# A decoder block on one core: sums, splits and the first gate put elsewhere in the mixing stage, one scaling moved to ScalarE

## The chip, the core and the metric

The kernel runs on one core of a Trainium2 chip. A core has TensorE (PE, matrix products; its weight loads are listed apart as PEld), VectorE (DVE), ScalarE (ACT), GpSimd (POOL) and SyncE (SP, which here issues nearly all DMA transfers). Each engine takes its instructions in order and waits for others through semaphores. Sixteen DMA engines move data between the chip's memory and the core's own.

The metric is the device time of one execution in microseconds (us), as the median of several runs. Beside it stands one profiled execution, from which all rows below come; a time such as "at 288.05" is counted from the start of that execution's span.

## What is computed

One decoder layer on 256 tokens of 1024 channels, in float32: a gated feed-forward network, a mixing layer of two branches, a second feed-forward network, a norm. Cut to what matters:

```python
h = h + 0.5 * swiglu(rmsnorm(h, ffn1_norm), ffn1_w_gate, ffn1_w_up, ffn1_w_down)
n = rmsnorm(h, mix_norm)
z = n @ w_in                         # q, k, v (512 each), u, gv (512 each)
attn = moba_attention(q, k, v)       # 8 heads of 64; 256 tokens are one block: causal softmax
zg = gelu(z[..., 3 * 512:])
gm = u * (tril(w_s) @ layernorm(gv) + b_s)      # by groups, inside chunks of 128 tokens
gates = sigmoid(n @ w_gate + b_gate)            # 2 x 1024 columns
merged = gates[:, :1024] * (attn @ w_branch_attn) + gates[:, 1024:] * (gm @ w_branch_gmlp)
h = h + merged @ w_out
h = h + 0.5 * swiglu(rmsnorm(h, ffn2_norm), ffn2_w_gate, ffn2_w_up, ffn2_w_down)
return rmsnorm(h, final_norm)
```

## The kernel before

**Split products.** A float32 product is made of three passes: each operand is split into a high part (rounded by a cast) and a low part (the rest), and high by high, high by low and low by high are summed in PSUM (`mm3`, L253). For the weights this is done on the chip. A weight *unit* comes as two *halves* of 512 KB. A half is loaded into a `raw` tile (`fetch_to`, L173; DMA on SP's queue), cast on ACT into the unit's tile `w` (L260), and its low part is subtracted on DVE (L262). I call the two steps *cast* and *low*. There are 7 raw tiles and 5 unit tiles, used in turn: the load of a half waits for the low of the half 7 before it, and a cast waits until PE has done with the unit 5 before it.

`split_half` (L185) takes the next half in the fixed order of units: it asks for loads up to six halves ahead, emits the cast, and either emits the low at once or, with `later=True`, returns it as a function that the caller runs at its own place. `unit(i, ahead)` (L221) takes halves until unit `i + ahead` is split, and then asks for one more load.

**Fewer products.** Some stages use sums of weight blocks so that seven products do the work of eight (`seven`, L385). Their units come in pairs: a "single" unit, and a "sums" unit that has no load of its own: four additions on DVE (L209 to L212) make its two halves from the raw tiles of the single one, which are then cast and lowered like others. `uvs` is such a stage: units `muv` to `muv + 3` hold the first half of u's and v's weights. The sums unit `muv + 3` is the last of them.

**Order.** From L752 on, the order of the program's text is the order on ACT and DVE (`in_order`), and it is so on PE and SP everywhere. A wait of one instruction holds all behind it on its engine. DMA transfers are issued by SP in the same way, in the order in which the text asks for them, loads of weights among them.

**The mixing stage** (L962 to L1067) runs, on PE, the products of q, k and gv, those of u and v, the scores (L863), the spatial products (L912), four *gate* chunks of 48 matmuls each (`chunk(mg, ...)`), the attention products (`attend`, L937), and two merges (`merge`, L1037), each with the gmlp branch (pg, L1041) and the attention branch (pa, L1052). Behind them stands the output product (`down_features`, acc, L229 and L234). On the other engines, in this stage:

- `turn_qk` (L845) scales q or k on ACT and turns it on DVE. The turned rows go to memory and come back in another layout (`qk_way`).
- `layer_norm(j)` (L949) on DVE, behind gv's gelu on ACT.
- `exponents(j)` (L873): maxima on DVE, exponents and their sums on ACT, for row tile j of 128 queries and 8 heads; tile 0 has 128 keys, tile 1 has 256.
- `probabilities(j, sm)` (L884): reciprocal of the sums, scaling of the whole tile (L890) and its turning (L893), all on DVE.
- `to_keys(j)` (L896) sends the turned probabilities to memory in four transfers, `by_keys(j)` (L901) brings them back by keys.
- `gated(i)` (L915): the spatial gating of half of the columns on DVE, and its turning; it leaves through `gm_way` and comes back as `gm_back`, from which `settle_in(gmT, gm_back)` (L1019) makes gm's high part on ACT and low part on DVE.
- `gate(g, ps, splits)` (L926): `2 * splits` halves are cast first, then for both row tiles gate g is scaled and added to its bias on DVE (L931) and put through the sigmoid on ACT (L933), then the lows run.
- `va` (L1007): v scaled on ACT.
- In `merge`, DVE multiplies by the gates (L1043, L1054), adds (L1055) and turns (L1056); the turned rows leave through `m_way`, come back, and `settle` (L1032) makes the high and low parts (mg) that the output product takes.

The gate units are `mg` to `mg + 7`. Behind them come the branches' units (gmlp, attention, gmlp, attention: `mb` to `mb + 3`) and the four of the output. Before the change, the halves of unit `mg + 5` are cast in `gate(0, psg, 1)`, those of `mg + 7` in `gate(1, ..., 1)`, those of `mb + 1` (the first attention branch) in `gate(2, ..., 1)`; the others by the `unit` calls of the chunks.

Of the kernel before, what the change touches and what calls it, by code (L numbers as in the profile page):

```python
# [10 lines left out]
F32 = mybir.dt.float32  # L11
F32R = mybir.dt.float32r
BF16 = mybir.dt.bfloat16
AF = mybir.ActivationFunctionType
# [4 lines left out]
P = 128  # L19
D = 1024  # L20
S = 256
NT = S // P
# [3 lines left out]
HEADS = 8  # L26
# [27 lines left out]
def block_kernel(ctx, tc, t, out):  # L54
    nc = tc.nc
# [84 lines left out]
    muv = len(units)  # L140
# [44 lines left out]
    def split_half(later=False):  # L185

        i, hf = divmod(done_to[0], 2)
        if hf == 0:
            unit_tile(i)
        fetch_to(done_to[0] + RAW)  # L190
        done_to[0] += 1
        if kind(i):
            return quarters(i, hf)
        w, sl = parts[i], half(i, hf)
        return split(w[:, sl, 0, :], w[:, sl, 1, :], raws.pop((i, hf)), later)

    def quarters(i, hf):

        w = parts[i]
        if kind(i) == "single":  # L200
            r = raws[i, hf].rearrange("p one (n c) -> p (one n) c", c=512)
            r, to = (r, w[:, 1:3]) if hf else (r[:, :1], w[:, :1])
        else:
            if hf == 0:
                (a, b), (c, d) = ([r[:, 0, n:n + 512] for n in (0, 512)] for r in [raws.pop((i - 1, k)) for k in range(2)])
                for k in range(2):
                    raws[i, k] = sump.tile([P, 2, 512], F32, tag="sum", name=f"sum{i}_{k}")
                first, second = raws[i, 0], raws[i, 1]
                nc.vector.tensor_add(first[:, 0], a, b)  # L209
                nc.vector.tensor_add(first[:, 1], b, d)  # L210
                nc.vector.tensor_add(second[:, 0], first[:, 0], d)
                nc.vector.tensor_add(second[:, 1], second[:, 0], c)  # L212
            r, to = raws.pop((i, hf)), w[:, 2 * hf:2 * hf + 2]
        return split(to[:, :, 0, :], to[:, :, 1, :], r)

# [356 lines left out]
    def by_token(way):  # L572
        return way.rearrange("(j p) a n -> p j (a n)", p=P)
# [178 lines left out]
    with in_order():  # L752
# [92 lines left out]
        def turn_qk(i, ps):  # L845
            by_tokens = tokens(mix_a[:, 8 + 4 * i:12 + 4 * i])
            for j in range(NT):
                nc.scalar.activation(by_tokens[:, j], ps[j], AF.Copy, scale=rs2[j])
                nc.vector.transpose(qk_turned[i][:, j], by_tokens[:, j])
# [33 lines left out]

        def probabilities(j, sm):  # L884


            n, pr = (j + 1) * P, prob[j]
            ri = small.tile([P, HEADS], F32, tag="ri", name=f"ri{j}")
            nc.vector.reciprocal(ri, sm)
            nc.vector.tensor_mul(pr, pr, ri[:, :, None].to_broadcast([P, HEADS, n]))  # L890
            turned.append(mix_a[:, 2 * KB:2 * KB + 4, :] if j == 0 else
                          act.tile([P, KB, S], F32, tag="nC", name="turned1"))
            nc.vector.transpose(turned[j].rearrange("p b (h c) -> p b h c", c=32),  # L893
                                pr.rearrange("p h (b c) -> p b h c", c=32))

        def to_keys(j):  # L896
            for b in range(4):
                nc.sync.dma_start(on_way[j][:, b, :].rearrange("(k r) n -> r k n", r=32),
                                  turned[j][32 * b:32 * (b + 1)])
# [23 lines left out]
            for j in range(NT):  # L923
                nc.vector.transpose(gm_turned[j][:, i * S:(i + 1) * S], m[:, j])

        def gate(g, ps, splits=0):  # L926

            c = slice(g * 512, (g + 1) * 512)
            lows = [split_half(True) for _ in range(2 * splits)]
            for j in reversed(range(NT)):  # L930
                nc.vector.scalar_tensor_tensor(gates[:, j, c], ps[j], rs2[j], gates[:, 0, c],  # L931
                                               op0=ALU.mult, op1=ALU.add)
                nc.scalar.activation(gates[:, j, c], gates[:, j, c], AF.Sigmoid)  # L933
            for low in lows:
                low()

# [28 lines left out]
        turn_qk(0, psq)  # L965
        chunk(mk, nT2, "k", 0, [1], psk, 3, DEEP)
        nc.sync.dma_start(by_token(qk_way[0]), qk_turned[0])
        turn_qk(1, psk)
        nc.sync.dma_start(by_token(qk_way[1]), qk_turned[1])
        q_back = tmp.tile([P, S // 32, P], F32, tag="back", name="qback", bufs=1)  # L970
# [25 lines left out]
        spatial()  # L996
        psg = chunk(mg, nT2, "g", 0, [0])
        nc.sync.dma_start(gates[:, 0, :], t["b_gate"].to_broadcast([P, 2 * D]))
        sums = [exponents(j) for j in range(NT)]
        gated(0)  # L1000
        probabilities(0, sums[0])
        to_keys(0)
        chunk(mg, nT2, "g", 0, [1], psg)
        probabilities(1, sums[1])
        gated(1)
        for j in range(NT):
            nc.scalar.activation(va[:, j, :], psv[j], AF.Copy, scale=rs2[j])  # L1007
        to_keys(1)
        by_keys(0)
        for j in range(NT):  # L1010
            nc.sync.dma_start(by_token(gm_way)[:, j], gm_turned[j])
        gate(0, psg, 1)
        psg = chunk(mg, nT2, "g", 1, [0])
        by_keys(1)
        gm_back = tmp.tile([P, S // 32, P], F32, tag="back", name="gmback", bufs=1)
        from_way(gm_back, gm_way)
        gate(1, chunk(mg, nT2, "g", 1, [1], psg), 1)
        gate(2, chunk(mg, nT2, "g", 2), 1)
        settle_in(gmT, gm_back)  # L1019
        gate(3, chunk(mg, nT2, "g", 3))  # L1020

# [221 lines left out]
```

## Time and profile before

| | |
|---|---|
| runs | 516.11, 516.30, 516.36 us |
| median | 516.3 us |
| the profiled execution | 516.4 us |
| its span | 514.7 us |
| mean granted clock of PE | 0.993 |

The span runs from the first to the last instruction; the 1.7 us around it are the execution's start and end. A row of a timeline gives start, length, engine, line of the program, operation, what it writes and reads, its shape and how many of the kind follow one another; a bracket at the end gives the engine's idle time before it and what ended it. A row of a group (with a bar) gives busy time, mean length in ns, and idle time before the group. A row of a stretch gives its bounds and length, then the busy time and number of instructions of PE, PEld, DVE, ACT and POOL, the granted clock of PE, the share of the 16 DMA engines that was busy, and GB/s. "SPq" is SP's queue of transfers: the time of a row is that of their issue, not of the landing.

### The profile page before, as it was taken

What the parts mean: (1) busy time and instruction counts of PE and PEld (TensorE: products, weight loads), DVE (VectorE), ACT (ScalarE), POOL (GpSimd) and SP (SyncE); (2) the same over time, 40 slices, a digit from 0 to 9 for tenths busy, and PEclk for the clock granted to TensorE, in tenths of its full rate; (3) what the DMA queues carried; (4) which work ended last, traced back from release to release, by engine and by line L of the source; (5) the groups of instructions that cost most, each with busy time, mean ns of one, the idle gap of its engine ahead of it and who ended that gap; (6) DMA issues with size and microseconds to landing.
All of it is one profiled execution on the core that took longest, in us unless ns stands there. A gap on an engine that the chain in (4) does not pass through costs nothing.

```text
span 514.7 us, 6830 instructions
## 1 busy us (share of the span) xinstructions
PE 505.0 (98%) x2314; PEld 418.7 (81%) x2314; DVE 462.1 (90%) x675; ACT 309.9 (60%) x444; POOL 11.2 (2%) x25
## 2 busy tenths in 40 slices
PE   9999999999999999999999999999999999999995
PEld 6888888888888888888888877888888888888884
DVE  6898999999997989799894876998989989999995
ACT  7985549646564766765952803768635756565533
POOL 0010000000000010000000000001000000000001
PEclk9999999999999999999999998999999999999998
DMA  8998588798765987786789765937789648998402
GB/s 317 375 330 327 156 276 258 267 307 280 228 220 179 308 282 291 184 291 245 232 218 304 287 202 171 295 120 260 257 274 300 213 140 274 350 327 251 177 1 82
DMA packets 63987, 126.82 MB, mean 246 GB/s; under 512 B 11729, under 2 KB 36817, under 8 KB 63825
## 3 DMA queue, kind: packets, MB, share of 16 engines
q1 hardware_dynamic: 63664, 126.06, 74.4%
q8 instruction: 18, 0.29, 0.3%
q10 hardware_dynamic: 288, 0.33, 0.2%
q14 instruction: 17, 0.13, 0.1%
HBM read 113.26 MB, written 13.11 MB: 246 GB/s over the span
## 4 chain that ended last, share of the span: by engine, by line
PE 94%; DVE 2%; DMA 2%; issue 1%; ACT 1%; SPq 0%; POOLq 0%; DVEq 0%; POOL 0%; ACTq 0%
PE f L255 12%; PE f L257 12%; PE f L256 12%; PE accdown L257 4%; PE accdown L255 4%; PE accdown L256 4%; PE acch L257 3%; PE acch L255 3%; PE acch L256 3%; PE acc L229 3%; PE g L255 3%; PE g L256 3%; PE g L257 3%; PE acc L234 1%; PE accuv L256 1%; PE accuv L257 1%
## 5 line engine op out<-in xcount | busy, mean ns | idle before, releaser
L262 DVE TENSOR_TENSOR w<-raw,w 128x1024 fp32r<-128x1024 f32 (+1 forms) x180 | 202.7, 1163 | 18.0 <-ACT w L260 17.6
L260 ACT CAST w<-raw 128x1024 fp32r<-128x1024 f32 (+1 forms) x180 | 173.2, 1007 | 31.4 <-DMA raw<-in_ba 8.3
L257 PE MATMUL f<-w,n 128*128 128x512 f32 x272 | 105.8, 389 | 0.0
L255 PE MATMUL f<-w,n 128*128 128x512 f32 x272 | 105.8, 389 | 0.0
L256 PE MATMUL f<-w,n 128*128 128x512 f32 x272 | 105.8, 389 | 0.0
L257 PEld LDWEIGHTS f<-w,n 128*128 128x128 f32 x272 | 51.1, 188 | 10.7
L256 PEld LDWEIGHTS f<-w,n 128*128 128x128 f32 x272 | 51.1, 188 | 10.6
L255 PEld LDWEIGHTS f<-w,n 128*128 128x128 f32 x272 | 51.1, 188 | 10.5
L260 ACT CAST w<-sum 128x1024 fp32r<-128x1024 f32 x34 | 35.8, 1052 | 37.6 <-DVE sum L210 29.5
L262 DVE TENSOR_TENSOR w<-sum,w 128x1024 fp32r<-128x1024 f32 x34 | 41.0, 1216 | 0.5 <-ACT w L260 0.5
L256 PE MATMUL accdown<-w,f1h 128*128 128x512 f32 x68 | 26.5, 389 | 0.0
L257 PE MATMUL accdown<-w,f1h 128*128 128x512 f32 x68 | 26.5, 389 | 0.0
L255 PE MATMUL accdown<-w,f1h 128*128 128x512 f32 x68 | 26.5, 389 | 0.0
L255 PE MATMUL g<-w,n 128*128 128x512 f32 x64 | 25.0, 391 | 0.0
L257 PE MATMUL g<-w,n 128*128 128x512 f32 x64 | 24.9, 389 | 0.0
L256 PE MATMUL g<-w,n 128*128 128x512 f32 x64 | 24.9, 389 | 0.0
L256 PE MATMUL acch<-w,f2h 128*128 128x512 f32 x59 | 23.0, 389 | 0.0
L257 PE MATMUL acch<-w,f2h 128*128 128x512 f32 x59 | 23.0, 389 | 0.0
L255 PE MATMUL acch<-w,f2h 128*128 128x512 f32 x59 | 23.0, 389 | 0.0
L229 PE MATMUL acc<-mg,w 128*128 128x512 f32 x64 | 18.7, 420 | 2.2 <-DVE mg L262 2.2
L596 ACT ACTIVATE f2s<-f,rstd 128x256 f32<-128x256 f32 x18 | 8.2, 474 | 14.0 <-PE f L257 13.9
L229 PEld LDWEIGHTS acc<-mg,w 128*128 128x128 f32 x64 | 12.2, 205 | 4.2 <-DVE mg L262 2.4
(291 smaller groups left out, 917.0 us busy)
## 6 DMA issues: line engine op xcount, KB each, us to landing
raw<-in_f SPq DMA_DIRECT2D x72, 512.0 KB, 6.5
raw<-in_f2d SPq DMA_DIRECT2D x22, 512.0 KB, 6.8
raw<-in_gate SPq DMA_DIRECT2D x16, 512.0 KB, 5.9
raw<-in_f1s SPq DMA_DIRECT2D x14, 512.0 KB, 6.4
raw<-in_f1d SPq DMA_DIRECT2D x14, 512.0 KB, 5.0
raw<-in_out SPq DMA_DIRECT2D x8, 512.0 KB, 5.3
raw<-in_f2s SPq DMA_DIRECT2D x6, 512.0 KB, 6.7
f1way<-f1t SPq DMA_DIRECT2D x11, 256.0 KB, 6.3
```

Source lines behind the costliest of these rows:

```text
L229: nc.tensor.matmul(ps, st, both.rearrange("p two n -> p (two n)"), start=first, stop=last)
L234: nc.tensor.matmul(ps[:, n:], st, both[:, 0, :], start=False, stop=False)
L255: nc.tensor.matmul(ps, sh, mh, start=first, stop=False)
L256: nc.tensor.matmul(ps, sh, ml, start=False, stop=False)
L257: nc.tensor.matmul(ps, sl, mh, start=False, stop=last)
L260: nc.scalar.copy(hi, src)
L262: nc.vector.tensor_sub(lo, src, hi.bitcast(F32))
L596: nc.scalar.activation(sg, ps[j][:, :CH], AF.Silu, scale=rs[j])
```

## The change

1. The four additions for the sums unit `muv + 3` become a function, `quarter_sums`, and are called by hand between k's product and k's turning; before, they were emitted behind the turning, with the split of that unit.
2. `probabilities(j)` keeps the reciprocal and the scaling. For tile 1 the scaling is eight activations on ACT, one for each head, in place of one multiplication on DVE. The turning is a function of its own, `turn(j)`.
3. `gate` is cut into `gate_in` (scaling and bias, DVE) and `gate_out` (sigmoid, ACT). For gate 0, `gate_in` stands ahead of the second tile's turning, and `gate_out` behind its way to the keys and ahead of `va`.
4. The halves of `mg + 4` are cast ahead of the exponents, those of `mg + 5` ahead of the second tile's scaling; their lows run behind the first and the second turning. `gate(2)` takes no halves any more, so the two of `mb + 1` are split with the next chunk, behind `settle_in` of gm.
5. `to_keys(1)` stands ahead of `va`.

```diff
+    def quarter_sums(i):
+        (a, b), (c, d) = ([r[:, 0, n:n + 512] for n in (0, 512)] for r in [raws.pop((i - 1, k)) for k in range(2)])
+        for k in range(2):
+            raws[i, k] = sump.tile([P, 2, 512], F32, tag="sum", name=f"sum{i}_{k}")
+        first, second = raws[i, 0], raws[i, 1]
+        nc.vector.tensor_add(first[:, 0], a, b)
+        nc.vector.tensor_add(first[:, 1], b, d)
+        nc.vector.tensor_add(second[:, 0], first[:, 0], d)
+        nc.vector.tensor_add(second[:, 1], second[:, 0], c)
...
-            if hf == 0:
...
+            if hf == 0 and (i, 0) not in raws:
+                quarter_sums(i)
...
-            n, pr = (j + 1) * P, prob[j]
+            pr = prob[j]
             ri = small.tile([P, HEADS], F32, tag="ri", name=f"ri{j}")
             nc.vector.reciprocal(ri, sm)
-            nc.vector.tensor_mul(pr, pr, ri[:, :, None].to_broadcast([P, HEADS, n]))
+            if j:
+                for hd in range(HEADS):
+                    nc.scalar.activation(pr[:, hd, :], pr[:, hd, :], AF.Copy, scale=ri[:, hd:hd + 1])
+            else:
+                nc.vector.tensor_mul(pr, pr, ri[:, :, None].to_broadcast([P, HEADS, P]))
+
+        def turn(j):
+
+            pr = prob[j]
             turned.append(mix_a[:, 2 * KB:2 * KB + 4, :] if j == 0 else
...
-        def gate(g, ps, splits=0):
+        def gate_in(g, ps):
 
             c = slice(g * 512, (g + 1) * 512)
-            lows = [split_half(True) for _ in range(2 * splits)]
             for j in reversed(range(NT)):
                 nc.vector.scalar_tensor_tensor(gates[:, j, c], ps[j], rs2[j], gates[:, 0, c],
                                                op0=ALU.mult, op1=ALU.add)
+
+        def gate_out(g):
+
+            c = slice(g * 512, (g + 1) * 512)
+            for j in reversed(range(NT)):
                 nc.scalar.activation(gates[:, j, c], gates[:, j, c], AF.Sigmoid)
+
+        def gate(g, ps, splits=0):
+
+            lows = [split_half(True) for _ in range(2 * splits)]
+            gate_in(g, ps)
+            gate_out(g)
             for low in lows:
                 low()
...
         nc.sync.dma_start(by_token(qk_way[0]), qk_turned[0])
+        quarter_sums(muv + 3)
         turn_qk(1, psk)
...
+        lows = [split_half(True) for _ in range(2)]
         sums = [exponents(j) for j in range(NT)]
         gated(0)
         probabilities(0, sums[0])
+        turn(0)
         to_keys(0)
+        for low in lows:
+            low()
         chunk(mg, nT2, "g", 0, [1], psg)
+        lows = [split_half(True) for _ in range(2)]
         probabilities(1, sums[1])
         gated(1)
+        gate_in(0, psg)
+        turn(1)
+        to_keys(1)
+        for low in lows:
+            low()
+        gate_out(0)
         for j in range(NT):
             nc.scalar.activation(va[:, j, :], psv[j], AF.Copy, scale=rs2[j])
-        to_keys(1)
         by_keys(0)
         for j in range(NT):
             nc.sync.dma_start(by_token(gm_way)[:, j], gm_turned[j])
-        gate(0, psg, 1)
         psg = chunk(mg, nT2, "g", 1, [0])
...
-        gate(2, chunk(mg, nT2, "g", 2), 1)
+        gate(2, chunk(mg, nT2, "g", 2))
         settle_in(gmT, gm_back)
         gate(3, chunk(mg, nT2, "g", 3))
```

More of the change, by code (lines that the diff above doesn't have):

```diff
@@ L203, in quarters @@
         else:
-            if hf == 0:
[L205 to L212, printed above, removed]
+            if hf == 0 and (i, 0) not in raws:
+                quarter_sums(i)
             r, to = raws.pop((i, hf)), w[:, 2 * hf:2 * hf + 2]
```

## The prediction

> **What bounds the kernel now.** I read the busy table first, then the rows in which TensorE (PE) idles, then the chain that released it, then the queues behind that chain.
>
> ```profile
> PE 505.0 (98%) x2314; PEld 418.7 (81%) x2314; DVE 462.1 (90%) x675; ACT 309.9 (60%) x444; POOL 11.2 (2%) x25
> ```
>
> PE is the bound, so a change to DVE, ACT or the queues pays only where PE waits. PE's timeline has one such place after the start (start, length, then idle before it):
>
> ```profile
> 307.50 0.28 PE L257 MATMUL pa<-w,ao 128*128 128x256 f32 x1
> 309.98 2.50 PE L229 MATMUL acc<-mg,w 128*128 128x512 f32 x5 [2.20 <-DVE mg L262]
> ```
>
> After the second merge's last matmul PE waits 2.20 us for the first settled block of the merged rows. The stretches around it (PE busy behind the first comma, granted clock third from the end) add a second cost:
>
> ```profile
> 306.27:309.68 3.41, 1.50 (x13) 1.30 (x11) 0.18 (x1) 0.62 (x2) 0.00 (x0) 1.00 0.59 134
> ```
> ```profile
> 309.68:313.09 3.41, 3.11 (x7) 2.48 (x8) 2.72 (x7) 2.10 (x5) 0.00 (x0) 0.50 0.81 235
> ```
>
> For the 3.41 us after the wait the clock is halved. Seven matmuls fill 3.11 us, 0.43 each, where L229 at full clock takes 3.84 us for 16 (quoted below), some 0.23 a piece: 7 x 0.2 = 1.4 us lost. Wait and clock are 3.6 us, 0.7% of the kernel; nothing else is to be had from PE here.
>
> The chain of waits says what the first block waited for:
>
> ```profile
> 302.27 2.96 DMA mway<-mt
> ...
> 306.67 2.29 DMA mixed<-mway
> 309.06 0.41 ACT mg L260
> 309.50 0.44 DVE mg L262
> ```
>
> The first merge leaves at 302.27 and comes back 7 us later, with DMA alone in between. Its end on DVE is late because DVE was late already; DVE's rows before it, then ACT's:
>
> ```profile
> 274.84 1.22 DVE L262 TENSOR_TENSOR w<-raw,w 128x1024 fp32r<-128x1024 f32 x1
> 282.65 1.22 DVE L262 TENSOR_TENSOR w<-raw,w 128x1024 fp32r<-128x1024 f32 x1 [6.59 <-ACT w L260]
> 284.63 1.22 DVE L262 TENSOR_TENSOR gm<-gmback,gm 128x1024 fp32r<-128x1024 f32 x1 [0.76 <-ACT gm L260]
> 285.77 2.35 DVE L262 TENSOR_TENSOR w<-raw,w 128x1024 fp32r<-128x1024 f32 x2
> 288.05 1.53 DVE L931 SCALAR_TENSOR_TENSOR mixed<-g,rstd,mixed 128x512 f32<-128x512 f32 x2
> ```
> ```profile
> 281.56 1.05 ACT L260 CAST w<-raw 128x1024 fp32r<-128x1024 f32 x1 [6.93 <-DMA raw<-in_ba]
> 282.52 1.15 ACT L933 ACTIVATE mixed<-mixed 128x512 f32<-128x512 f32 x2
> 283.57 1.03 ACT L260 CAST gm<-gmback 128x1024 fp32r<-128x1024 f32 x1
> ```
>
> DVE idles 6.59 us, then is late for 20 us: the cast at 281.56 waited for a half of the attention branch's weights, and the gated rows (gm) and gate 3 (288.05) stood behind it. From 288.05 to 302.25 DVE is nearly gapless. The clock of the wait thus starts in the DMA queue:
>
> ```profile
> 258.70 3.07 SPq L898 DMA_DIRECT2D on_way<-turned  x4
> ...
> 269.55 2.15 SPq L570 DMA_DIRECT2D gmback<-gmway  x4
> ```
> ```profile
> 275.00:280.00 5.00, 5.00 (x24) 4.14 (x23) 1.06 (x1) 0.00 (x0) 0.00 (x0) 1.00 1.10 234
> ```
> ```profile
> DMA to landing us min/median/max: 8.7/9.2/9.3
> ```
>
> The last row is of gmback. Its last transfer was issued at 271.2 and landed 9.3 later, at 280.5, since the 16 DMA engines were full (share 1.10). I call 280.5 G.
>
> **The change, part by part.** *Sums ahead of k's turning (quarter_sums).*
>
> ```profile
> 208.06 1.39 DVE L849 STREAM_TRANSPOSE mixed<-mixed 128x512 f32<-128x512 f32 x2 [2.02 <-ACT mixed L848]
> 209.37 0.65 DVE L209 TENSOR_TENSOR sum<-raw 128x512 f32<-128x512 f32 x1
> ```
> ```profile
> 210.72 1.05 ACT L260 CAST w<-sum 128x1024 fp32r<-128x1024 f32 x1 [2.01 <-DVE sum L210]
> ...
> 213.06 1.28 ACT L979 ACT_TABLE_LOAD   x1
> ```
> ```profile
> 213.03 0.39 PE L257 MATMUL gv<-w,n 128*128 128x512 f32 x1
> ```
> ```profile
> 215.07 0.69 DVE L951 BATCH_NORM_STATS2 st<-mixed 128x6 f32<-128x512 f32 x1 [0.77 <-ACT mixed L979]
> ```
>
> The four adds (0.63 apart, 2.5 us) fill DVE's 2.02 us of idleness and push k's turning, and on SP's queue k's way out and the first gate loads behind it, by 0.4; these are cover, since the scores that need k run behind uv, at 234 (below). ACT's two casts no longer wait 2.0 for the sums and end by 210.7 instead of 213.0. The layer norm then waits for PE's gv (213.4, its first rows 0.7 sooner) instead of the table load: 213.45, 1.6 before 215.07. DVE is full behind it, so the -1.6 reaches the uv results. PE gains there as well: the scores' last eight matmuls wait for banks that those results hold. The same number take 0.87, then 1.57:
>
> ```profile
> 234.74:235.61 0.87, 0.87 (x13) 0.67 (x9) 1.00 0.87 344
> 235.61:237.18 1.57, 1.57 (x10) 0.88 (x8) 1.00 0.79 261
> ```
>
> I take 0.6 (bounds 0 and 0.7). It makes PE reach the wait sooner, at 307.15 instead of 307.8, and so is worth nothing until the chain is faster too.
>
> *The second row tile's scaling on ACT.* No row of before has this form. The nearest, same width and a scale by partition, is L322; the exponents with their read-outs are the upper end:
>
> ```profile
> 193.00 1.71 ACT L322 ACTIVATE n<-h,cols 128x256 fp32r<-128x256 f32 x4 [0.54 <-DMA h<-hway]
> ```
> ```profile
> 236.75 1.17 ACT L869 COPY mixed<-sc 128x256 f32<-128x256 f32 x4
> ```
> ```profile
> L880 ACT ACTIVATE mixed<-mixed,nm 128x128 f32<-128x128 f32 (+1 forms) x16 | 7.0, 442 | 2.3 <-DVE nm L877 2.3
> ```
> ```profile
> 254.03 2.30 DVE L890 TENSOR_TENSOR mixed<-mixed,ri 128x2048 f32<-128x2048 f32 x1
> 256.36 2.31 DVE L893 STREAM_TRANSPOSE turned<-mixed 128x2048 f32<-128x2048 f32 x1
> ```
>
> Four L322 take 1.71, with the last one's own half microsecond in it, so they start 0.41 apart and eight cost 3.3 on ACT. Sixteen exponents, half of them narrower, take 7.0, 0.44 each: 3.5 for eight, and 3.9 is my upper bound, since all eight are wide; 2.4 is the lower, from L869's 0.3 each, copies without a scale. I take 3.3, from the row with the same width and the same kind of scale. DVE loses the 2.30 of L890. The table load for the sigmoids and the two va copies stand behind the scaling on ACT; nothing needs them before 261. On DVE the second half of gated and the first gate (1.9 and 1.5) fill the time meanwhile. My order of events follows both engines. ACT: the casts behind the scores' copies start at 237.2 (0.6 sooner, with PE's scores); there are four now, 0.95 apart, then the table load of 1.28, so the exponents start at 242.4 instead of 243.4 and end, 7.0 later, at 249.4; two more casts, then the scaling, 251.3 to 254.6. DVE: two lows, the maxima, gated's first half, the first tile's scaling and turning, all as long as before, end at 248.9 instead of 250.3; two lows to 251.1, the reciprocal, gated's second half and the first gate, to 254.6. The turning then runs 254.7 to 257.0 instead of 256.36 to 258.67. The scaling is free only up to 3.3; at the upper end the turning is 0.6 later.
>
> The Trainium skill (ScalarE: Activation LUTs, "Rules for kernel authors") speaks against this step: multiplications belong on VectorE, and an activation costs about 0.3 us and 0.83 ns an element. That would be an estimated 4.1 us for the eight, the keys 0.8 later, PE released at 309.5 with its clock lost: 515.9. The trace gives 0.41 for the same width, and the multiplication's saving here is DVE's time, not its price, so I keep 3.3.
>
> *Two units cast sooner, and where their lows and loads go.* The lows stay off the turnings: behind the first and behind the second one, 1.14 apart. On SP, one load now waits ahead of each to_keys; ahead of the second it is a 512 KB load that waits for the first low behind the turning, so SP stands until 258.2, and the four transfers to keys follow at 258.6 (before 258.70). That load no longer stands behind gmway. From there to G the set of transfers is the same; the queue starts 0.4 sooner and, fed by a large load, with fewer holes. I take G 0.5 sooner, 280.0 (bounds: 0.8 later, if the keys pay for half of that load, and 1.2 sooner).
>
> *Gate 2 without splits.* The half cast at 281.56 now stands behind gm. From G on: gm's cast 1.03, then on DVE gm and four halves at 1.14, all loads of which land in time (281.5 and 1.3 apart), and gate 3 at G + 6.8. Before it started at 288.05, G + 7.6. That is 0.8 sooner at the same G; the half whose low stood at 274.84 is added, the 1.1 us of waiting behind the branch's weights and the sigmoids' slot are saved.
>
> *Sum.* Gate 3 and all behind it 0.8 + 0.5 = 1.3 sooner: PE released at 308.7. It arrives at 307.15, so the wait shrinks from 2.2 to 1.5. PE would be busy for 1.9 of the 3.41 us that ended with the drop, where it was busy for 1.50; I take it that the clock then stays up, and another 1.4 is won (bounds: -0.15, below, and 1.4). Next late is the third pair of blocks:
>
> ```profile
> 320.99 0.71 ACT L260 CAST mg<-mixed 128x256 fp32r<-128x256 f32 x2 [7.30 <-DMA mixed<-mway]
> ```
> ```profile
> 322.68 3.84 PE L229 MATMUL acc<-mg,w 128*128 128x512 f32 x16
> ```
>
> PE, 2.7 sooner, wants it at 320.0; the cast, 1.3 sooner, ends at 320.1: some 0.2 given back. Later DVE, 1.3 sooner, must not hold PE, 2.5 sooner; it has 2.19 of idleness to catch up in:
>
> ```profile
> 413.24 0.69 DVE L432 TENSOR_TENSOR f2p<-accf2p,f2p 128x512 f32<-128x512 f32 x1 [2.19 <-issue]
> ```
>
> The Trainium skill (TensorE: Matmul & The Clock Gate, "What's actually happening") halves the clock after an idle window of about 3.4 us, counted by windows that run freely. Taken so, a wait of 1.5 us costs no clock at all, which is the sum below; by the same rule 2.2 us would have cost none either, and there the trace disagrees.
>
> Gain 1.3 + 1.4 - 0.2 = 2.5. The profiled execution took 516.4 (span 514.7), 0.1 above the median of 516.3: **513.8**.
>
> **The rivals.** *The clock still drops.* All of the shorter wait lies in the stretch 306.27 to 309.68, and no row shows from which busy time on the clock is kept. If it falls, PE runs 1.0 at full clock, then the whole 3.41 at half: 1.55 lost instead of 1.4, gain 1.3 - 0.15, 515.1. For it: the runs of 516.11 to 516.36 and the profiled 516.4 lie closer than 1.4, so the drop comes each time. Against it: 1.9 is over half of the stretch, 1.50 under it.
>
> *Gm comes no sooner.* The queue is full for 20 us whatever the order. With G at 280.5 to 281.3 the gain is 0.8 to 0, PE's 0.6 only lengthens the wait, and the clock falls: 515.6 to 516.4.
>
> *Slower: the big load ahead of the keys.* to_keys, by_keys and gmback follow one another on one queue. If the 512 KB (1.3 us when the queue is full) pushes the keys and the keys' return pushes gmback again, G passes 282.3; from 281.3 on the kernel loses. At G + 2.5 PE's release comes at 311.7: 516.3 + 1.7 = 518.0. Against it: the load was in the same stretch before, only later.
>
> *The wait nearly goes.* With G 1.2 sooner, at its bound, PE is released 2.0 sooner and the clock stays up: 516.3 - 2.0 - 1.4 + 0.1 = 513.0; a still shorter wait reaches 512.7.
>
> **How the numbers follow.** Forecast 0.47, clock drops 0.28, gm no sooner 0.14, slower 0.07, the wait nearly gone 0.04. The range runs from 512.7 to 516.3. A measurement here tells 0.2%, 1.0 us, from no change, so faster means below 515.3: forecast, the wait nearly gone and two thirds of the clock rival, 0.70; same 0.23; slower 0.07.
>
> **What would show it.** Right: layer norm's statistics at 213.5; no gap in the last scores; turning of tile two ending near 257; gmback landed near 280; gate 3 near 286.8; a PE wait before L229 of about 1.5 with the clock at 1.00 behind it. Wrong: 0.50 in the stretch behind the wait; gate 3 at 288 or later; a new PE wait in the merges or at L229 past 315.

## The result, and the profile after

| | before | after |
|---|---|---|
| median of 22 runs each | 515.84 us | 513.03 us |
| lowest to highest | 514.31 to 517.44 | 511.68 to 516.54 |
| after over before | | 0.9949 [0.9936, 0.9963] |
| the profiled execution | 516.4 | 512.95 |
| its span | 514.7 | 511.2 |

The change is worth 0.51% [0.37, 0.64], 2.6 us; the forecast of 513.8 is 0.8 above the median. In a second comparison the ratio was 0.9961 [0.9943, 0.9979].

The PE waits of the kernel after (who waited for whom; total, times, longest) are these three:

```profile
PE warm L105 <- DVE zeros L102: 1.2, 1, 1.2
PE f L701 <- ACT n L677: 0.5, 1, 0.5
PE acc L232 <- DVE mg L265: 0.3, 1, 0.3
```

The wait in front of the output product has gone from 2.20 to 0.33 us. (L232, L263, L265, L940 are before's L229, L260, L262, L931.) The two stretches around it, in TensorE's own steps of 3.41 us, show PE busy 3.08 and 3.41, and the granted clock (third from the end) 1.00 in both, where before it was 0.50 behind the wait:

```profile
304.54:307.95 3.41, 3.08 (x24) 2.82 (x23) 1.02 (x3) 0.71 (x2) 0.00 (x0) 1.00 0.60 132
307.95:311.36 3.41, 3.41 (x20) 2.92 (x19) 2.93 (x6) 2.62 (x4) 0.00 (x0) 1.00 0.86 297
```

The timeline of DVE, and that of ACT, hold the chain that leads there:

```profile
213.46 0.69 DVE L971 BATCH_NORM_STATS2 st<-mixed 128x6 f32<-128x512 f32 x1 [1.46 <-ACT mixed L1000]
...
254.63 2.31 DVE L903 STREAM_TRANSPOSE turned<-mixed 128x2048 f32<-128x2048 f32 x1 [0.20 <-ACT mixed L894]
...
280.09 1.23 DVE L265 TENSOR_TENSOR gm<-gmback,gm 128x1024 fp32r<-128x1024 f32 x1 [7.25 <-ACT gm L263]
281.23 4.62 DVE L265 TENSOR_TENSOR w<-raw,w 128x1024 fp32r<-128x1024 f32 x4
285.77 1.53 DVE L940 SCALAR_TENSOR_TENSOR mixed<-g,rstd,mixed 128x512 f32<-128x512 f32 x2
```
```profile
251.30 3.30 ACT L894 ACTIVATE mixed<-mixed,ri 128x256 f32<-128x256 f32 x8
...
279.01 1.05 ACT L263 CAST gm<-gmback 128x1024 fp32r<-128x1024 f32 x1 [5.50 <-DMA gmback<-gmway]
```

The statistics come 1.6 earlier, the turning 1.7 earlier, and gm's cast, which now waits for nothing but the landing G, starts at 279.01. So G is 278.9, 1.6 sooner than the 280.5 of before. That is not because the keys went out sooner. SP's rows have them at 258.52, where before has 258.70:

```profile
258.12 0.35 SPq L183 DMA_DIRECT2D raw<-in_bg  x1
258.52 3.34 SPq L908 DMA_DIRECT2D on_way<-turned  x4
```

What has become shorter is the time from there to G. The DMA view of exactly this stretch, of before and then of after (packets, what they moved, rate; the queue's share of the 16 engines), and the last line on gmback's four transfers in after:

```profile
DMA packets 3413, 5.59 MB, mean 257 GB/s; under 512 B 259, under 2 KB 2307, under 8 KB 3412
...
q1 hardware_dynamic: 3412, 5.58, 95.3%
```
```profile
DMA packets 3401, 5.56 MB, mean 273 GB/s; under 512 B 255, under 2 KB 2303, under 8 KB 3400
...
q1 hardware_dynamic: 3400, 5.54, 96.9%
```
```profile
DMA to landing us min/median/max: 6.7/7.3/7.6
```

The engines are full nearly all the way, and the same 5.6 MB took 21.8 us before and 20.4 after; gmback's last transfer landed 7.6 instead of 9.3 us after its issue. The shares split the gain: 95.3% of 21.77 us is 20.75 of work, 96.9% of 20.39 is 19.76. So of the 1.6, about 1.0 is less work for the engines, 0.4 is less idleness between transfers, and 0.2 is the earlier issue.

**Where the time went,** between the two profiled executions. PE was ready for the output product at 307.77 before and is at 307.08 (307.41 less the wait): -0.69. The wait: -1.87. From the product's first matmul to the first one behind it (f):

```profile
333.85 0.39 PE L255 MATMUL f<-w,n 128*128 128x512 f32 x1
```
```profile
307.41 2.14 PE L232 MATMUL acc<-mg,w 128*128 128x512 f32 x8 [0.33 <-DVE mg L265]
...
311.26 0.63 PE L237 MATMUL acc<-mg,w 128*128 128x256 f32 x4
311.90 0.73 PE L232 MATMUL acc<-mg,w 128*128 128x512 f32 x2
...
318.51 0.63 PE L237 MATMUL acc<-mg,w 128*128 128x256 f32 x4
319.15 1.19 PE L232 MATMUL acc<-mg,w 128*128 128x512 f32 x4
...
330.42 0.39 PE L258 MATMUL f<-w,n 128*128 128x512 f32 x1
```

Before that is 309.98 to 333.85, 23.87; after 307.41 to 330.42, 23.01. A kernel below, with no stall there, takes 22.33. So before lost 1.54 to the clock, and after loses 0.68 to short stalls: four matmuls of 256 columns take 0.64 from start to next start (311.26 to 311.90, 318.51 to 319.15) where 0.47 would do, as PE has caught up with the settled blocks. The stalls are not new: the kernel before in an execution without a fall (below) takes 22.90, 0.57 of it lost in the same way. In all -0.69 - 1.87 - 1.54 + 0.68 = -3.4, of 3.5 in the spans.

This is more than the medians' 2.6, because the profile of before shows a fallen clock and most runs have none, as the next section shows.

### The profile page after: what moved, and what is told of

It reads as the page before. It is cut to its first block, busy times and chain, and to the rows that moved or that the text cites. A ratio compares the mean times of both kernels' runs of the same rounds, so it can differ in the third digit from the quotient of the medians.

```text
span 511.2 us, 6831 instructions
## 1 busy us (share of the span) xinstructions
PE 503.0 (98%) x2314; PEld 417.1 (82%) x2314; DVE 459.1 (90%) x674; ACT 312.3 (61%) x452; POOL 11.4 (2%) x25
## 4 chain that ended last, share of the span: by engine, by line
PE 90%; DMA 3%; DVE 3%; issue 1%; ACT 1%; SPq 0%; POOLq 0%; DVEq 0%; POOL 0%; ACTq 0%
PE f L260 12%; PE f L259 12%; PE f L258 12%; PE accdown L260 4%; PE accdown L259 4%; PE accdown L258 4%; PE acch L260 4%; PE acch L259 4%; PE acch L258 3%; PE acc L232 3%; PE g L258 2%; PE g L259 2%; PE g L260 2%; DMA raw<-in_bg 2%; PE acc L237 1%; DVE w L265 1%
## 5 line engine op out<-in xcount | busy, mean ns | idle before, releaser
L265 DVE TENSOR_TENSOR w<-raw,w 128x1024 fp32r<-128x1024 f32 (+1 forms) x180 | 202.5, 1162 | 9.2 <-ACT w L263 9.0
L263 ACT CAST w<-raw 128x1024 fp32r<-128x1024 f32 (+1 forms) x180 | 172.2, 1007 | 20.2 <-PE f L260 7.5
L260 PE MATMUL f<-w,n 128*128 128x512 f32 x272 | 105.8, 389 | 0.0
L260 PEld LDWEIGHTS f<-w,n 128*128 128x128 f32 x272 | 51.1, 188 | 10.5
L263 ACT CAST w<-sum 128x1024 fp32r<-128x1024 f32 x34 | 35.7, 1052 | 36.8 <-DVE sum L203 28.1
L265 DVE TENSOR_TENSOR w<-sum,w 128x1024 fp32r<-128x1024 f32 x34 | 40.9, 1215 | 0.5 <-ACT w L263 0.5
L260 PE MATMUL accdown<-w,f1h 128*128 128x512 f32 x68 | 26.5, 389 | 0.0
L260 PE MATMUL g<-w,n 128*128 128x512 f32 x64 | 24.9, 389 | 0.0
L260 PE MATMUL acch<-w,f2h 128*128 128x512 f32 x59 | 23.0, 389 | 0.0
L232 PE MATMUL acc<-mg,w 128*128 128x512 f32 x64 | 17.5, 398 | 0.4 <-DVE mg L265 0.3
L263 ACT CAST mg<-mixed 128x256 fp32r<-128x256 f32 x8 | 2.9, 404 | 20.3 <-DMA mixed<-mway 20.2
## 6 DMA issues: line engine op xcount, KB each, us to landing
raw<-in_f SPq DMA_DIRECT2D x72, 512.0 KB, 6.1
raw<-in_f2d SPq DMA_DIRECT2D x22, 512.0 KB, 7.0
raw<-in_gate SPq DMA_DIRECT2D x16, 512.0 KB, 6.5
raw<-in_f1s SPq DMA_DIRECT2D x14, 512.0 KB, 6.5
raw<-in_f1d SPq DMA_DIRECT2D x14, 512.0 KB, 5.2
raw<-in_out SPq DMA_DIRECT2D x8, 512.0 KB, 5.2
raw<-in_f2s SPq DMA_DIRECT2D x6, 512.0 KB, 6.7
```

Source lines behind the costliest of these rows:

```text
L232: nc.tensor.matmul(ps, st, both.rearrange("p two n -> p (two n)"), start=first, stop=last)
L260: nc.tensor.matmul(ps, sl, mh, start=False, stop=last)
L263: nc.scalar.copy(hi, src)
L265: nc.vector.tensor_sub(lo, src, hi.bitcast(F32))
```

## The experiments

In each the theories are told by what they make of G, of the wait (before 2.2, after 0.3) and of the median. The kernels of one set ran on one chip beside before; there are three sets: the first four with a median of before of 515.37 (35 runs), the next four with 515.25 (29), the last four with 515.27 (24).

**The clock: before, unchanged.**

> The kernel of before, unchanged, with the mean granted clock of each run. The 22 runs of before spread from 514.3 to 517.4 us, though the profiled execution and three runs lay within 0.3. Theory A (the clock's windows run freely against the program, and the 2.2 us wait costs the clock only where one window holds enough of it): the runs fall in two groups some 1.5 to 2 us apart, and the mean clock of the slow group is lower by about 0.003 (half of 3.41 us out of 515). Rival B (the spread comes from transfers): no relation between time and mean clock.

515.47 us, ratio 1.0007 [0.9990, 1.0024]. Its profile has a wait of 2.26 (308.70 to 310.96), and no fall. (G is 1.0 later in this execution, and PE also waits 0.53 for gm ahead of the first merge, so a late G costs at two places.) In steps of 3.41 us, counted from the moment at which this execution's clock rose (5.75 us; 5.89 in the first profile of before, whose fall at 309.68 is 89 steps of 3.413 later):

```profile
306.12:309.54 3.42, 2.58 (x22) 2.38 (x20) 0.00 (x0) 0.00 (x0) 0.00 (x0) 1.00 0.38 88
309.54:312.95 3.41, 1.99 (x9) 1.65 (x10) 2.14 (x6) 1.93 (x5) 0.00 (x0) 1.00 0.68 176
```

The border of the steps cuts this wait into 0.84 and 1.42, and the clock stays. In the first profile 1.91 of the wait lay in one step, and it fell. So it falls by what one step holds. The ends of the executions, where PE runs out of work, narrow the limit. The step in which PE ends its work, and the one behind it, in the profiles of two experiments below, of gate 2 without splits and of the second tile scaled on DVE:

```profile
505.15:508.56 3.41, 1.52 (x13) 1.32 (x11) 2.23 (x8) 1.34 (x6) 1.04 (x3) 1.00 0.39 154
508.56:511.97 3.41, 0.00 (x0) 0.00 (x0) 0.67 (x2) 0.60 (x1) 0.00 (x0) 0.50 0.42 154
```
```profile
507.15:510.56 3.41, 1.57 (x14) 1.37 (x12) 2.26 (x7) 1.38 (x5) 1.04 (x3) 1.00 0.39 153
510.56:513.97 3.41, 0.00 (x0) 0.00 (x0) 0.68 (x2) 0.61 (x1) 0.00 (x1) 1.00 0.43 154
```

PE busy for 1.52 of a step loses the clock, 1.57 keeps it, and no step of the 14 profiles contradicts that: the limit lies between 1.84 and 1.89 us of idleness in one step.

In all 14 each fall comes a whole number of steps after the clock's rise, and the rise itself comes anywhere from 3.85 to 7.20 us: where the steps lie changes from run to run. A fall costs 3.41 x 0.5 / 514 = 0.0033 of the mean clock, and so nearly always shows in it, since executions profiled without one have 0.996 to 0.999. Of 88 runs of before in the three sets 20 have a mean clock of 0.995 or less (median 516.75), the other 68 have 515.1. The kernel after fell once in 22 runs and once in 12. The three runs shown before the forecast, 516.11 to 516.36, fit either group. What the waits were in the runs without a profile isn't known, so how often the clock should fall can't be worked out.

**The clock: no wait at all.** Nine products whose result nobody reads fill the wait:

```diff
         merge(1)
+        fill = bank("fill")
+        for i in range(9):
+            nc.tensor.matmul(fill, gmT[:, 0, 0, :P], gmT[:, 0].rearrange("p two n -> p (two n)"), start=True, stop=True)
```

> The kernel of before with nine products of 512 columns, whose result nobody reads, ahead of the output product: 2.1 us of work for PE inside its wait of 2.2. Theory A (the slow group of runs is the halved clock after the wait): the wait stays as long for the output product, at 309.98, but the clock stays at 1.00 behind it in every run; the slow group vanishes, median 514.4 to 514.8 against 515.8 of before. Rival B (the groups have another cause): two groups as before, median unchanged.

515.83 us, ratio 1.0010 [0.9997, 1.0022]. The clock half holds: no run of 11 has a mean clock under 0.996, where 20 of 88 would make it two or three. The median half is a miss. The fill takes 2.1 us:

```profile
308.14 2.23 PE L1072 MATMUL fill<-gm 128*128 128x512 f32 x9
310.21 1.07 PE L229 MATMUL acc<-mg,w 128*128 128x512 f32 x4
```

and where a run's wait would have been shorter than that, the fill itself holds PE. The saved falls are worth 20/88 x 1.65 = 0.4 us on average, and the median doesn't show them; that the fill gave them back is argued, not shown.

**One part alone.** The sums ahead of k's turning (`quarter_sums` and its call, nothing else), and gate 2 without splits:

```diff
-        gate(2, chunk(mg, nT2, "g", 2), 1)
+        gate(2, chunk(mg, nT2, "g", 2))
```

> The kernel of before with the four additions of the last uv sums put ahead of k's turning, and nothing else of the change. Theory A (the layer norm waited for the table load behind these sums; DVE is full up to the turnings): statistics of the layer norm at 213.5 instead of 215.1, exponents from 242.0 instead of 243.4, turning of the second tile ends at 257.2 instead of 258.7, gated rows landed at 279.1 instead of 280.5, gate 3 on DVE from 286.6, PE at the wait at 307.1 and released at 308.5: wait 1.4, median about 514.0 to 514.4. Rival B (the later DMA queue is full anyway, so it hides the gain): gated rows land at 280.5 and gate 3 stays at 288.0; the wait grows to 2.8 and the time stays within 0.3 of before.

> The kernel of before with no halves split in gate 2, so that the first attention half stands behind the gated rows' settling; nothing else of the change. Theory A (0.8 us come from this order alone): gated rows landed at 280.5 as before, gate 3 on DVE 6.8 us behind that, at 287.3 instead of 288.05, PE released at 309.2, wait 1.4; median about 0.8 to 1.5 below before, the upper figure where the clock is kept more often. Rival B (one more half behind the gated rows costs as much as the wait for the weights cost): gate 3 at 288.0 or later, no gain.

Sums: 514.38 us, ratio 0.9982 [0.9967, 0.9996]. Gate 2: 514.54, ratio 0.9987 [0.9973, 1.0000], an interval that ends at no change. Both medians are where theory A had them. Their rows:

```profile
213.41 0.69 DVE L954 BATCH_NORM_STATS2 st<-mixed 128x6 f32<-128x512 f32 x1 [0.77 <-ACT mixed L983]
...
308.44 1.89 PE L232 MATMUL acc<-mg,w 128*128 128x512 f32 x7 [1.42 <-DVE mg L265]
```
```profile
281.69 1.23 DVE L262 TENSOR_TENSOR gm<-gmback,gm 128x1024 fp32r<-128x1024 f32 x1 [6.58 <-ACT gm L260]
282.83 4.62 DVE L262 TENSOR_TENSOR w<-raw,w 128x1024 fp32r<-128x1024 f32 x4
287.37 0.75 DVE L931 SCALAR_TENSOR_TENSOR mixed<-g,rstd,mixed 128x512 f32<-128x512 f32 x1
...
309.18 1.20 PE L229 MATMUL acc<-mg,w 128*128 128x512 f32 x4 [0.89 <-DVE mg L262]
```

The sums bring the statistics from 215.07 to 213.41 and leave a wait of 1.42. That wait lies whole in one step of the clock (305.30 to 308.71), which stays up. Without the splits the row from the landing (280.51) to gate 3 is 6.86 instead of 7.6, and the wait 0.89; the 1.4 expected was a miss, as PE came 0.5 later in this execution.

**One part undone,** in the kernel after: the early sums; gate 2's splits put back; the second row tile scaled on DVE as before, in the new order.

```diff
-        quarter_sums(muv + 3)
```
```diff
-        gate(2, chunk(mg, nT2, "g", 2))
+        gate(2, chunk(mg, nT2, "g", 2), 1)
```
```diff
-            if j:
-                for hd in range(HEADS):
-                    nc.scalar.activation(pr[:, hd, :], pr[:, hd, :], AF.Copy, scale=ri[:, hd:hd + 1])
-            else:
-                nc.vector.tensor_mul(pr, pr, ri[:, :, None].to_broadcast([P, HEADS, P]))
+            nc.vector.tensor_mul(pr, pr, ri[:, :, None].to_broadcast([P, HEADS, (j + 1) * P]))
```

> The kernel after without the early sums of the value weight: they stand again behind the turning of k, as in the kernel before. Theory A (they delay the layer norm's statistics by 1.6 us and all that follows to the gm product's landing by nearly as much, and TensorE at the scores by 0.6): statistics at about 215.1, turning at about 256.1, landing at 279.9 to 280.9, gate 3 at 286.8 to 287.8, TensorE ready at about 307.7, the last product waits 0.6 to 1.5 us, median 513.9 to 514.6. Rival B (DMA takes the shift up): landing within 0.4 of 278.9, wait 0 to 0.3, and only the 0.6 us of TensorE lost, median 513.3 to 513.8.

> The kernel after with the two splits ahead of gate 2 put back. Theory A (they lengthen DVE's gapless row between the landing and gate 3 by 0.8 us): gate 3 stands 7.6 us behind the landing instead of 6.86, at about 286.5, the last product's operand is there at about 308.2, it waits 0.9 to 1.2 us instead of 0.3, median 513.5 to 514.0. Rival B (the row has slack; the splits are paid elsewhere in any order): gate 3 within 0.2 of 285.8 behind an equal landing, wait 0.2 to 0.5, median within 0.2 of the kernel after.

> The kernel after, with the second row tile's probabilities scaled by one DVE product as in the kernel before, the order otherwise kept. Theory A (the scaling on ACT beside DVE's gate work carries the turning forward by its whole length, and each microsecond at the keys is one at the gm product's landing): turning at 256.5 to 257 instead of 254.6, keys at about 260.7, landing at 281.0 to 281.8, gate 3 at 287.9 to 288.7, the last product waits 2.2 to 3.0 us, median 514.9 to 515.6. Rival B (the earlier sums alone carry the gain, ACT's scaling is hidden anyway): landing at most 0.5 later than in the kernel after, wait at most 0.8, median 512.8 to 513.6.

| without | median | ratio to before | G | gate 3 | wait |
|---|---|---|---|---|---|
| early sums | 514.24 | 0.9979 [0.9966, 0.9993] | 280.9 | 287.80 | 0.72 |
| gate 2 plain | 514.08 | 0.9978 [0.9961, 0.9996] | 277.8 | 285.43 | 0 |
| ACT's scaling | 514.23 | 0.9983 [0.9964, 1.0001] | 282.5 | 289.36 | 2.23 |

By their ratios to before (the kernel after was not in this set) each of the three gives back about half of the gain; the intervals don't rank them, and the last includes no change. The late sums came out as their theory had it, to half a microsecond at each point. With the splits back, the row to gate 3 is 7.59 again, as expected, but the profiled execution was that kernel's shortest (512.43), with an early landing, so its wait tells nothing; the median is 0.1 above the theory's band, and three of the twelve runs have a mean clock of 0.995 or less. With the scaling on DVE, the turning follows it:

```profile
252.13 2.29 DVE L892 TENSOR_TENSOR mixed<-mixed,ri 128x2048 f32<-128x2048 f32 x1
...
257.60 2.30 DVE L899 STREAM_TRANSPOSE turned<-mixed 128x2048 f32<-128x2048 f32 x1
```

The profile shows what the theory said (a turning 3.0 later, a wait of 2.23). About 0.9 of the 3.0 is not the scaling's: DVE was that late in this execution ahead of the maxima already, though statistics and scores were as early as in after. PE also waits 1.20 for the attention's operand (ao) in the first merge, as the keys go out only at 261.44. But this is one of its longest runs (516.61), and the median of 514.23 is below the 514.9 to 515.6 expected: the size was a miss. This profile gives one more point on the clock: 1.69 of the wait in one step, and it stays:

```profile
309.18:312.59 3.41, 1.72 (x8) 1.43 (x9) 1.81 (x5) 1.60 (x5) 0.00 (x0) 1.00 0.67 174
```

**Why G came sooner than forecast.** The trace has each packet's time. The keys' four writes are 1024 packets of 1 KB. Their mean was 69 ns before and 52 after, though the same tiles go the same way (the expectations below have 68 and a difference of 16, rounded down); 1024 x 17 ns over 16 engines is 1.1 us of all of them, and they are nearly full from the keys to G, as shown. All other packets of the stretch took as much as before, 16.4 us of the 16 engines then and 16.5 after. What differs on the queue is the 512 KB load directly ahead. So the load was put behind the keys in the kernel after (for the first row tile too):

```diff
+        hold[0] = fetched[0]
         lows = [split_half(True) for _ in range(2)]
...
         to_keys(1)
+        hold[0] = None
+        fetch_to(done_to[0] + RAW - 1)
```

and, the other way round, a load was put ahead of the keys in the kernel before:

```diff
         probabilities(1, sums[1])
+        for low in [split_half(True) for _ in range(2)]:
+            low()
         gated(1)
...
-        gate(0, psg, 1)
+        gate(0, psg)
```

> The kernel after, with one thing moved back: the 512 KB weight load that it issues ahead of the keys' writes is issued behind them, the keys' own issue staying at about 258.5. Theory A (the gm product's landing came 1.1 us sooner than forecast because the keys' 1 KB packets move faster when a large load is queued ahead of them on the same queue: 52 ns each in the kernel after against 68 ns in the kernel before): the packets are back at 64 to 69 ns, the landing stands 21.3 to 22.8 us behind the keys' first issue instead of 20.4, so at about 280.0 to 281, gate 3 at about 286.8 to 287.8, the last product waits 1.0 to 2.0 us for its operand instead of 0.3, median 513.6 to 514.4. Rival B (the earlier turning alone brought the landing forward, and the packets' mean is a matter of what else runs then): packets at 50 to 56 ns, landing 278.5 to 279.3, wait 0 to 0.6, median within 0.3 of the kernel after.

> The kernel before, with the two splits of gate 0 moved ahead of DVE's product of the gate of v, so that one 512 KB load is issued ahead of the keys' writes of the second row tile and holds these until its buffer is free. Theory A (a load of the same queue ahead of them makes the keys' packets cheaper, 1024 of them by 16 ns over 16 engines, so 1.0 us): the keys go out at about 260.2 instead of 258.7, their packets take 50 to 55 ns, the landing stands 20.0 to 21.0 us behind their first issue instead of 21.8 to 22.8, at 280.2 to 281.2, median within 0.5 of the kernel before. Rival B (the packets' time hangs on something else in the order of the kernel after): packets 64 to 70 ns, landing 281.7 to 283, wait above 3 us, median 0.6 or more above the kernel before.

From the packets and the issues in the traces:

```
                 load     keys out  mean of 1024  G        G - keys  MB moved
                                    packets (ns)                     between
before           behind   258.70    69            280.47   21.8      5.59
before, again    behind   258.66    69            281.49   22.8      5.74
load ahead       ahead    260.26    52            279.12   18.9      5.27
after            ahead    258.52    52            278.91   20.4      5.56
after, again     ahead    259.50    52            279.24   19.7      5.49
loads behind     behind   256.89    68            277.90   21.0      5.40
loads behind 2   behind   256.89    68            278.16   21.3      5.63
```

The packets' time follows the load in both directions, as the theory had it: 52 with a load ahead, 68 to 69 without. The stretch to G follows less sharply: in the seven other profiles it is 19.4 to 21.1 with a load ahead and 20.7 to 21.7 without, so the groups touch, with means over all 14 of 20.0 and 21.5. But the load's place does a second thing, which the expectation had missed by holding the keys' issue at 258.5. Ahead of them, the load waits for its buffer, and SP with it; behind them, the keys go 1.6 us sooner, as soon as the turning ends:

```profile
256.89 3.07 SPq L908 DMA_DIRECT2D on_way<-turned  x4
260.07 1.26 SPq L183 DMA_DIRECT2D raw<-in_bg  x1
```

That outweighs the dearer packets. The first of these kernels took 512.27 us, ratio 0.9940 [0.9924, 0.9957], less than either theory gave; its profile has no wait before the output product. The load ahead in the kernel before brought 515.36 us, ratio 0.9996 [0.9979, 1.0014]: there the keys go out 1.5 later, and the medians don't differ. Its profile's G of 279.12 and wait of 0.65 are better than that, with only 5.27 MB between: one execution's G spreads by a microsecond (after 278.91, again 279.24, and 277.84 in the kernel with gate 2's splits, the same program up to there), so one profile tells the packets' time well and the median badly.

**Side by side, and a version that turns at once.** On one chip: the kernel after; the loads behind the keys; and the latter with the scaling on DVE and the turning directly behind it:

```diff
         probabilities(1, sums[1])
-        gated(1)
-        gate_in(0, psg)
         turn(1)
         to_keys(1)
+        gated(1)
+        gate_in(0, psg)
```

> The kernel after, unchanged, for the spread of its landing, of its wait and of its clock beside the others on one chip. Theory A (the wait before the output product is what the landing leaves of it, and the clock falls only where the wait fills enough of one of TensorE's 3.41 us windows): the gm product's landing between 277.8 and 279.5, wait 0 to 0.9 us, no fall of the clock, no run below a mean clock of 0.996, median 0.4 to 0.65% below the kernel before. Rival B (the after profile was a lucky one): landing above 280, wait above 1.2 us, several runs below 0.996, median less than 0.35% below.

> The kernel after with the weight loads issued behind the keys' writes, a second time, beside the kernel after on the same chip. Theory A (the keys go out 1.6 us sooner since they no longer stand behind a load that waits for its buffer, their packets cost 1.0 us more of all DMA engines, and what is left is 0.6 us and more at the landing): keys at about 256.9, packets 66 to 70 ns, landing 277.4 to 278.4, no wait, median 0.3 to 0.9 us below the kernel after. Rival B (both are as good, the wait is gone in both): medians within 0.3 us.

> The kernel of the loads behind the keys, and the second row tile's probabilities scaled on DVE and turned directly behind it, ahead of DVE's product of the gate of v and of the first gate's addition. Theory A (what counts is where the turning ends, not which engine scales; behind that nothing waits for the gate's addition): turning at about 253.5 to 255.8, 1.1 sooner than with ACT's scaling, keys at 255.8, landing 276.4 to 277.6, no wait, median within 0.4 of the loads_again kernel, since no wait is left to take. Rival B (DVE's row behind the turning is then too late, and gate 1 to 3 or the keys' product pay for it): gate 3 no sooner than 284.8, the wait back at 0.5 or more, median 0.5 or more above loads_again.

| | median | ratio to before | turning | G | gate 3 |
|---|---|---|---|---|---|
| after, again | 513.31 | 0.9961 [0.9943, 0.9979] | 255.61 | 279.2 | 286.11 |
| loads behind the keys | 512.01 | 0.9932 [0.9907, 0.9957] | 254.55 | 278.2 | 285.03 |
| and turned at once, on DVE | 511.87 | 0.9930 [0.9906, 0.9955] | 253.69 | 276.7 | 283.60 |

The kernel after repeats its result, at 0.38% just under the expected gain of 0.4%. Its profile has no wait this time; one run of twelve fell (0.993), where none was expected. The loads behind the keys are 1.3 us better in the median, more than the 0.3 to 0.9 expected. All six runs lie within 511.70 and 512.58, and the highest is below eleven of the twelve of the kernel after, and 0.18 above its lowest. PE's row has neither wait nor stall left:

```profile
306.69 0.28 PE L260 MATMUL pa<-w,ao 128*128 128x256 f32 x1
306.81 2.00 PE L232 MATMUL acc<-mg,w 128*128 128x512 f32 x8
```

and the output product takes 22.33 (306.81 to 329.14). In the third kernel the chain is 1.4 us sooner again and the median the same, as expected: there is no wait to take any more. It also shows that with the loads behind the keys ACT's scaling is not needed:

```profile
251.36 2.29 DVE L892 TENSOR_TENSOR mixed<-mixed,ri 128x2048 f32<-128x2048 f32 x1
253.69 2.31 DVE L899 STREAM_TRANSPOSE turned<-mixed 128x2048 f32<-128x2048 f32 x1
...
283.60 1.53 DVE L936 SCALAR_TENSOR_TENSOR mixed<-g,rstd,mixed 128x512 f32<-128x512 f32 x2
```

What the change needed was the turning ahead of DVE's 3.3 us of gating, or an engine for the scaling beside it; it took the second.

## Why the prediction was right, and where it was not

- **The bound** was the right one. Between the two profiles all is gained at the one wait, where PE also comes 0.69 sooner, and in the clock behind it; kernels without that wait (512.0, 511.9) gain nothing from a still faster chain.
- **Sums:** statistics at 213.45, measured 213.46; alone 213.41, undone 215.55. PE's 0.6: measured 0.69.
- **ACT's scaling** at 3.3: measured 3.30, and the turning at 254.63 where 254.7 was forecast. The Trainium skill's rule (ScalarE: Activation LUTs, "Rules for kernel authors"), an estimated 4.1 us for the eight, does not hold for the row: one of them took the 0.50 us that the rule gives, but they start 0.40 apart and overlap, so that eight took 3.30.
- **The load ahead of the keys:** SP free for the keys at 258.6, measured 258.52. But I saw in it only something to be hidden or to be paid for. It was both a price of 1.6 us of SP and a gain of 1.1 us of the DMA engines.
- **The step that failed** is "I take G 0.5 sooner, 280.0". It came 1.6 sooner, 0.4 beyond the lower bound of 1.2. What that step counted was right: the same set of transfers, an earlier issue (0.2 measured) and fewer holes (0.4). What it left out is the packets' price: it took the keys' packets as in before, and they cost 1.1 us less. With it gate 3 moved by 2.3 (288.05 to 285.77) and the release by 2.6 instead of 1.3, and the wait shrank to 0.33 instead of 1.5.
- **From G on:** gate 3 at G + 6.8, measured 6.86; with the splits 7.6, measured 7.55 to 7.59. This term is right.
- **The clock:** it stayed up, as forecast. The reason given against that, "the drop comes each time", was false: it comes in 20 of 88 runs. The reason for it, that 1.9 is over half of the stretch and 1.50 under it, was close: the limit lies between 1.52 and 1.57 busy. The rival's 1.55 for a whole step at half clock should have been 3.41 x 0.5 = 1.7. So the 1.4 (1.54 in the profile) is a gain against the profiled execution, but 0.4 on the average of runs. The Trainium skill (TensorE: Matmul & The Clock Gate, "What's actually happening") has windows of 3413 ns that run freely, and all 14 profiles agree with this. Its rule of one idle window does not fit a fall after 1.91 or 1.89 us of idleness out of 3.41. The prediction saw that disagreement, but not that it turned on where the window lay.
- **Given back:** 0.2 forecast at the third pair; 0.68 measured: 0.3 there, as much at the second pair, and 0.1 at the first product. The kernel before had 0.57 of such stalls when its clock did not fall, so little of this was new.
- **The rivals.** The wait nearly went; its price, 513.0, is the median, and I gave it 0.04. The forecast of 513.8 is nearer than its steps, because two misses had opposite signs: a chain forecast 1.3 too late, and a clock counted as if every run had lost it. That is luck. Gm did come sooner, the clock did not fall, and the big load did not push G back.

Two things stay open. Why a load ahead makes the packets cheaper was not tried. The DMA engines stand all but idle in the last microsecond before the keys go out (share 0.00 to 0.02), with a load ahead or without; with it the load's packets come first and the keys' behind them. Whether that takes a large load, or any transfer directly ahead, no run tells. And the parts' shares are known only to about a microsecond, since G itself spreads by as much.

## What to carry to other kernels

Where a chain of small transfers decides a wait, count what stands between its issue and its landing: here the engines were full nearly all the way, so the landing moved with the sum of the packets' times and with the issue, not with the engine work ahead. Before shifting work to another engine, look at what stands behind the last step in its own engine's order, and at what load holds its queue. And before a clock loss is counted as a gain, look at the mean clock of several runs: a loss in one profile may be a loss in one run out of four.

## What the hardware showed

- TensorE's clock changed only at the borders of steps of 3.41 us, counted from its first rise, in all fourteen profiles. A step with 1.84 us or less of idleness kept it, one with 1.89 or more lost it for the next step.
- Writes of 1 KB packets took 52 to 53 ns each with a 512 KB load issued directly ahead on their queue, 68 to 69 ns without, in all fourteen profiles.
